# Sums of weight blocks made pair by pair, raw buffers reused in the order they come free, one bias load on another queue

## The chip, the core and the metric

The kernel runs on one core of a Trainium2 chip. The metric is the device time of one execution in microseconds (us). The kernel before was run three times; a fourth execution was profiled.

## What is computed

A streaming encoder with two layers, 512 frames of 1024 features, all in fp32. Cut to what matters here:

```
for i in range(DEPTH):                       # 2 layers
    h = rmsnorm(x, norm1_g[i])
    z = h @ w_in[i] + b_in[i]                # q, k, v, o, gates of an mLSTM; q, k, v, g of a retention; two branch gates
    y_m = sigmoid(mo) * headnorm(mlstm(mq, mk, mv, mi, mf))
    y_r = silu(rg) * headnorm(retention(rope(rq), rope(rk), rv))
    x += (sigmoid(gm) * (y_m @ w_bm[i]) + sigmoid(gr) * (y_r @ w_br[i])) @ w_out[i]
    x += relu(rmsnorm(x, norm2_g[i]) @ w_ff1[i] + b_ff1[i]) ** 2 @ w_ff2[i] + b_ff2[i]
    x += sigmoid(rmsnorm(x, norm3_g[i]) @ w_pe_gate[i]) * (p[i] @ w_pe[i])
return rmsnorm(x, final_g)
```

## The kernel before

**Products.** Activations lie transposed: features on the 128 partitions, 512 frames along the row. Each fp32 factor is split into a high and a low part (`split`, L286: a copy on ScalarE gives the high part, a subtraction on VectorE the low one), and a product is three matmuls: high by high, high by low, low by high. All weights are streamed from HBM once. `unit_list` (L152) writes out by hand the order of 302 units, 151 per layer. A T8 unit is a 1024x128 slice of weights for one output tile (24 matmuls of 512 columns), four V units are a 1024x512 slice for values, and PAIR and WIDE units are 2x2 blocks of weights that are multiplied by a scheme with seven block products in place of eight. That scheme needs, beside the four given blocks B11, B12, B21 and B22, the sums t1 = B12 + B11 and t3 = B12 + B22, and for WIDE also t2 = t1 + B22 (`MADE`, L96).

**Sums of weights.** t1, t2 and t3 are made in HBM by DMAs that GpSimd issues. `groups` (L128) puts PAIR units that belong together into a group of four (of two in the group `gm`); each WIDE unit is a group of its own. `sum_steps` (L315) lists, for each of the 24 groups in the order of their use, a copy of the first block into the sum (`a` = 0) and an accumulating DMA of the second one (`a` = 1), each over the whole group: t1 copy, t3 copy, t1 add, t3 add, for WIDE also t2 copy and t2 add. A group of four pairs or a WIDE group moves 1 MB in one step, the group `gm` 512 KB. The rows of a transfer lie on 128 rows of the block (`flat`, L312) and are cut at 4096 bytes. `step` (L327) issues the next one and makes it wait for the last matmul handed out until then. `tick` (L336) decides when: each unit adds a credit worked out from its time and its own load (`TIME`, L107; T8 and V units count 5.45 us), and while the credit is not negative, a step is issued for 4.5 of credit per MB. `next_unit` (L343) calls it once per unit, `run_wide` (L510) also inside the unit.

**Loads.** `fill_raws` (L363) hands out the loads of raw weights in the order of use on SyncE's queue: 512 KB for T8, V and WIDE pieces, twice 256 KB for a PAIR piece. A raw tile has 128x1024 elements. Four of them rotate under one tag (`wr`, `RAWS` = 4), so that load n + 4 of that tag waits for the tile of load n. One more (`wrx`), in the pool `low`, is used for units before `w_out` of the running layer, one load at a time (`cur["more"]`). `prep_next` (L391) fills raws, then splits the next piece into its high and low parts; in PAIR units it also forms differences and sums in the raw tiles (L423, L426), and in WIDE units L430. `ready` (L433) keeps this two units ahead of the product (`LOOK`, `READY`). Loads, splits and products have a fixed order on each engine; a late load holds the splits behind it on ScalarE and VectorE.

**Around them.** `t8` (L448), `run_pair` (L474) and `run_wide` (L510) issue the matmuls of a unit. `values` (L741) computes mLSTM values; its bias row, spread over 128 partitions, is loaded on SyncE's queue (L744) into a temporary tile (six of them rotate), and VectorE adds it at L727. GpSimd's queue also carries the spill and the fetch of retention values (L1177, L1207), the loads of x before `w_out` (L1363), the causal masks of the mLSTM (L1032), the powers of the norms (L667, L1052, L1098) and the sums of squares (L653). `Norm.square` (L637) holds the sum of squares in a tile `ssum`, `Norm.spread` (L701) the spread factor in a tile `rb`, 128x512 each, in the pool `one`. At the start, 11 matmuls on a tile of ones (L915, `WARM`) precede the first product.

Of the kernel before, what the change touches and what calls it, by code (L numbers as in the profile page):

```python
# [35 lines left out]
F32 = mybir.dt.float32  # L36
# [16 lines left out]
UN = 1024  # L53
LOOK = 2
AHEAD = 250
WARM = 11
NTMP = 6
RAWS = 4
PIECES = 3
# [59 lines left out]
def is_wide(g):  # L119
    return g[1][:2] == "rv"  # L120
# [116 lines left out]
def build(ctx, tc, ins, out):  # L237
# [71 lines left out]
    def block(g, x):  # L309
        return given[g, x] if x in GIVEN else sums[g, x]  # L310

    def flat(a):  # L312
        return a.rearrange("a p q -> (a p q)").rearrange("(r w) -> r w", r=P)

    def sum_steps():  # L315

        out = []
        for g in index:
            out += [(g, "t1", 0), (g, "t3", 0), (g, "t1", 1), (g, "t3", 1)]
            if is_wide(g):  # L320
                out += [(g, "t2", 0), (g, "t2", 1)]
        return out

    steps = sum_steps()
    made = {g: 0 for g in index}

    def step():  # L327
        g, x, a = steps[at["step"]]
        at["step"] += 1
        made[g] += 1  # L330
        kw = {"accum_op": OP.add} if a else {}
        dma = gp.dma_start(flat(block(g, x)), flat(block(g, MADE[x][a])), max_dma_last_dim=4096, **kw)
# [21 lines left out]
    formed = {}  # L354

    room = unit_list(0).index(("T8", "w_out", 0, 0))
    cur["room"], cur["more"] = (), None

    def halves(n):

        return [slice(0, Q), slice(Q, UN)] if n == 1 else [slice(0, UN)]

    def fill_raws(most=RAWS + 1):  # L363
        while at["load"] < len(loads) and len(raws) + len(kept) < most:
            n, x = loads[at["load"]]
            r = None
            if n in cur["room"] and cur["more"] not in raws:
                cur["more"] = n, x
                r = cur["low"].tile([P, UN], F32, name=f"wr{at['load']}", tag="wrx", bufs=1)
            elif len(raws) - (cur["more"] in raws) >= RAWS:  # L370
                break
            raws[n, x] = r = r or wpool.tile([P, UN], F32, name=f"wr{at['load']}", tag="wr", bufs=RAWS)
            if x:
                _, g, p = units[n]
                assert made[g] == 2 * len(MADE_OF(g)), (g, made[g], at["unit"])
                if is_wide(g):
                    in_order("load", nc.sync.dma_start(r, block(g, x[0])[x[1]]))
                else:
                    for k, y in enumerate(PIECE[x]):
                        in_order("load", nc.sync.dma_start(r[:, k * Q:(k + 1) * Q], block(g, y)[p]))  # L380
            elif units[n][0] == "IF":
                eng = nc.sync if n else nc.scalar
                eng.dma_start(r[:, 0:64], ins["wif"][n * L // NU])
            else:
                w = ins["wstream"][at["whole"]]
                for c in halves(n):
                    in_order("load", nc.sync.dma_start(r[:, c], w[:, c]))
                at["whole"] += 1
            at["load"] += 1

    def prep_next():  # L391
        n, x = order[at["prep"]]
        at["prep"] += 1
        fill_raws()

        w = Q if x == "D" else UN
        pl = cur["last"] if n >= NU - LAST else wpool
# [20 lines left out]
        pieces[n, x] = out_  # L418
        if x == "A" or wide and x[0] == "t2":
            kept[n, x] = r  # L420
        elif x == "C":

            ve.tensor_tensor(raws[n, "B"][:, Q:], kept.pop((n, "A"))[:, Q:], r[:, :Q], OP.add)  # L423
        elif x == "B":

            ve.tensor_tensor(r[:, :Q], r[:, :Q], r[:, Q:], OP.add)  # L426
            formed[n, "D"] = r
        elif wide and x[0] == "B21":
            t = cur["br"].tile([P, UN], F32, name=f"t4{n}_{x[1]}", tag=("ph", "pl")[x[1]])
            ve.tensor_tensor(t, kept.pop((n, ("t2", x[1]))), r, OP.add)  # L430
            formed[n, ("t4", x[1])] = t

    def ready(k):  # L433
        while at["prep"] < min(len(order), k + 1):
# [39 lines left out]
    def run_pair(name, act, done):  # L474
# [5 lines left out]
        def product(x):  # L480
# [8 lines left out]
            for k in range(4):  # L489
# [4 lines left out]
                te.matmul(o, wh[:, s], l, start=False, stop=False, skip_group_check=True)  # L494
                cur["mm"] = te.matmul(o, wl[:, s], h, start=False, stop=e, skip_group_check=True)
            done(x, o)

        def last():
            product("P4")
# [113 lines left out]
    class Norm:  # L613


        def __init__(self, name, i, gain, act=None, j0=0, j1=NT):
# [20 lines left out]
        def square(self, k, x, add=None):  # L637
            w = self.n * P
            x = x[:, self.s]
            if self.sum is None:  # L640
                pl = cur["last"] if self.half else opool
                sq = pl.tile([P, w if self.half else T], F32, name=f"{self.name}sum", tag="ssum", bufs=1)[:, :w]
            else:
                sq = tmp(f"{self.name}sq{k}")[:, :w]
            ac.activation(sq, x, AF.Square)
# [55 lines left out]
        def spread(self):  # L701
# [11 lines left out]
            pl = cur["last"] if self.half else opool  # L713
# [198 lines left out]
    cur["room"] = range(room)  # L912
    n1 = Norm("l0n1", 0, "g1", acts(xa_pool, "l0n1"))
    warm = ps("warm")
    for _ in range(WARM):  # L915
# [14 lines left out]
    for i in range(L):  # L930
        act_side, ph_side = ("right", "left") if i == 0 else ("left", "right")
        xa = n1.act
        if i:
            cur["low"] = phase(f"low{i}", ph_side)
            cur["tmp"], cur["ntmp"] = cur["low"], NTMP
            cur["room"] = range(i * NU // L, i * NU // L + room)
        cur["br"] = phase(f"br{i}", ph_side)

        sel = cur["br"].tile([P, H, P], F32R, name=f"l{i}sel", tag="sel")[0:32 + H]
# [511 lines left out]
            ff1(b, p)  # L1451
        n2_pool.release()
        n3_pool = phase(f"n3{i}", act_side)
        n3 = Norm(f"l{i}n3", i, "g3", acts(n3_pool, f"l{i}n3"))


        pe = n3_pool.tile([P, KT, T], F32, name=f"l{i}pe", tag="pe")
# [26 lines left out]
        nn = ([Norm(f"l{i}n4{a}", i, "gf", None, 2 * a, 2 * a + 2) for a in range(2)] if last  # L1484
              else [Norm(f"l{i + 1}n1", i + 1, "g1", acts(xa_pool, f"l{i + 1}n1"))])

        def pe_evac(o, c, s, nn):
            w = s.stop - s.start
# [201 lines left out]
```

## Time and profile before

| | us |
|---|---|
| three runs | 2342.51, 2340.75, 2342.23 |
| median | 2342.23 |
| profiled execution, device time | 2342.72 |
| its span in the profile | 2341.0 |

Between the profiled execution's time and its span lie 1.7 us. The profile names engines PE (TensorE), PEld (its weight loads), DVE (VectorE), ACT (ScalarE), POOL (GpSimd) and SP (SyncE, which only issues DMAs); `L288` is line 288 of the kernel. Tiles carry the names of the program: `wr` is a raw tile of weights, `wh` and `wl` its parts, `s0t` to `s23t` the sums of the 24 groups, `l0` and `l1` the layers. DMA queue q0 is GpSimd's, q1 SyncE's, q10 ScalarE's. A row of the timeline gives start, duration, engine, line, what is written and read, the number of merged instructions, and in brackets the idle time before it with what ended it.

### The profile page before, as it was taken

What the parts mean: (1) busy time and instruction counts of PE and PEld (TensorE: products, weight loads), DVE (VectorE), ACT (ScalarE), POOL (GpSimd) and SP (SyncE); (2) the same over time, 40 slices, a digit from 0 to 9 for tenths busy, and PEclk for the clock granted to TensorE, in tenths of its full rate; (3) what the DMA queues carried; (4) which work ended last, traced back from release to release, by engine and by line L of the source; (5) the groups of instructions that cost most, each with busy time, mean ns of one, the idle gap of its engine ahead of it and who ended that gap; (6) DMA issues with size and microseconds to landing.
All of it is one profiled execution on the core that took longest, in us unless ns stands there. A gap on an engine that the chain in (4) does not pass through costs nothing.

```text
span 2341.0 us, 35229 instructions
## 1 busy us (share of the span) xinstructions
PE 2320.0 (99%) x13660; PEld 2055.5 (88%) x13660; DVE 1722.4 (74%) x2658; ACT 1223.2 (52%) x1771; POOL 243.5 (10%) x369
## 2 busy tenths in 40 slices
PE   9999999999999999999999999999999999999998
PEld 8788898898998898899888888998989988998997
DVE  7777766886675677678778777778957656776785
ACT  6756544554554445445557564454636445445464
POOL 2111100001002100001311110000000020000012
PEclk9999999999999999999999999999999999999999
DMA  6666776566688667777776645434343543432441
GB/s 207 172 175 161 227 221 197 183 197 204 181 235 266 191 199 194 197 215 189 203 219 175 173 129 185 139 119 158 122 144 110 161 153 99 127 108 92 136 124 54
DMA packets 146631, 394.89 MB, mean 169 GB/s; under 512 B 15376, under 2 KB 18832, under 8 KB 146464
## 3 DMA queue, kind: packets, MB, share of 16 engines
q1 hardware_dynamic: 99952, 247.77, 32.0%
q0 software_dynamic: 31104, 117.45, 20.8%
q10 hardware_dynamic: 15408, 27.43, 3.5%
q8 instruction: 107, 1.75, 0.3%
q14 instruction: 60, 0.49, 0.1%
HBM read 373.71 MB, written 123.73 MB: 212 GB/s over the span
## 4 chain that ended last, share of the span: by engine, by line
PE 87%; DVE 5%; issue 4%; DMA 2%; ACT 1%; POOL 0%; DVEq 0%; ACTq 0%; POOLq 0%; SPq 0%
PE l1f L444 2%; PE l0f L444 2%; PE l0f L445 2%; PE l1f L445 2%; PE l1f L446 2%; PE l0f L446 2%; PE l0br L444 1%; PE l1br L444 1%; PE l0br L446 1%; PE l1br L445 1%; PE l1br L446 1%; PE l0br L445 1%; DMA wr<-wpairs 1%; PE l0pg L444 1%; PE l1bm L444 1%
## 5 line engine op out<-in xcount | busy, mean ns | idle before, releaser
L287 ACT ACTIVATE wh<-wr 128x1024 fp32r<-128x1024 f32 (+1 forms) x223 | 231.2, 1043 | 282.3 <-issue 71.6
L288 DVE TENSOR_TENSOR wl<-wr,wh 128x1024 fp32r<-128x1024 f32 (+1 forms) x221 | 272.2, 1233 | 76.5 <-ACT wh L287 74.9
L287 ACT ACTIVATE wh_B<-wr 128x1024 fp32r<-128x1024 f32 x100 | 105.9, 1059 | 153.4 <-PE l0bm L445 13.1
L288 DVE TENSOR_TENSOR wl_B<-wr,wh_B 128x1024 fp32r<-128x1024 f32 x100 | 122.0, 1220 | 27.2 <-ACT wh_B L287 27.1
L287 ACT ACTIVATE wh_D<-wr 128x512 fp32r<-128x512 f32 x76 | 47.9, 631 | 127.5 <-DVE wr L426 67.6
L287 ACT ACTIVATE wh_C<-wr 128x1024 fp32r<-128x1024 f32 x76 | 80.3, 1056 | 63.6 <-issue 10.5
L288 DVE TENSOR_TENSOR wl_A<-wr,wh_A 128x1024 fp32r<-128x1024 f32 x76 | 92.8, 1221 | 20.2 <-ACT wh_A L287 20.2
L288 DVE TENSOR_TENSOR wl_C<-wr,wh_C 128x1024 fp32r<-128x1024 f32 x76 | 94.3, 1241 | 15.7 <-ACT wh_C L287 15.3
L287 ACT ACTIVATE wh_A<-wr 128x1024 fp32r<-128x1024 f32 x76 | 80.0, 1052 | 46.1 <-PE l1f L445 6.7
L444 PE MATMUL l0f<-l0n2h,wh 128*128 128x512 f32 x256 | 99.8, 390 | 0.0
L444 PE MATMUL l1f<-l1n2h,wh 128*128 128x512 f32 x256 | 99.8, 390 | 0.0
L446 PE MATMUL l1f<-l1n2h,wl 128*128 128x512 f32 x256 | 99.7, 389 | 0.0
L446 PE MATMUL l0f<-l0n2h,wl 128*128 128x512 f32 x256 | 99.7, 389 | 0.0
L445 PE MATMUL l0f<-l0n2l,wh 128*128 128x512 f32 x256 | 99.6, 389 | 0.0
L445 PE MATMUL l1f<-l1n2l,wh 128*128 128x512 f32 x256 | 99.6, 389 | 0.0
L288 DVE TENSOR_TENSOR wl_D<-wr,wh_D 128x512 fp32r<-128x512 f32 x76 | 52.4, 690 | 36.9 <-ACT wh_D L287 35.7
L423 DVE TENSOR_TENSOR wr<-wr,wr 128x512 f32<-128x512 f32 x76 | 52.1, 686 | 13.5 <-DMA wr<-wpairs 12.1
L446 PEld LDWEIGHTS l1f<-l1n2h,wl 128*128 128x128 f32 x256 | 48.0, 188 | 10.2
L446 PEld LDWEIGHTS l0f<-l0n2h,wl 128*128 128x128 f32 x256 | 48.0, 188 | 10.2
L444 PEld LDWEIGHTS l0f<-l0n2h,wh 128*128 128x128 f32 x256 | 48.1, 188 | 9.8
L445 PEld LDWEIGHTS l1f<-l1n2l,wh 128*128 128x128 f32 x256 | 48.1, 188 | 9.8
L444 PEld LDWEIGHTS l1f<-l1n2h,wh 128*128 128x128 f32 x256 | 48.1, 188 | 9.7
(5625 smaller groups left out, 8359.6 us busy)
## 6 DMA issues: line engine op xcount, KB each, us to landing
wr<-wstream SPq DMA_DIRECT2D x219, 512.0 KB, 4.3
wr<-wpairs SPq DMA_DIRECT2D x228, 256.0 KB, 2.9
wr<-wwide SPq DMA_DIRECT2D x24, 512.0 KB, 3.8
s0t<-wwide POOLq DMA_DIRECT2D x5, 1024.0 KB, 8.4
s4t<-wwide POOLq DMA_DIRECT2D x5, 1024.0 KB, 8.7
s12t<-wwide POOLq DMA_DIRECT2D x5, 1024.0 KB, 8.3
s16t<-wwide POOLq DMA_DIRECT2D x5, 1024.0 KB, 8.9
s1t<-wpairs POOLq DMA_DIRECT2D x4, 1024.0 KB, 8.1
```

The source lines that it names most:

```text
L287: a = ac.activation(hi_ap, src, AF.Copy)
L288: return a, ve.tensor_sub(lo_ap, src, hi_ap.bitcast(F32))
L423: ve.tensor_tensor(raws[n, "B"][:, Q:], kept.pop((n, "A"))[:, Q:], r[:, :Q], OP.add)
L444: te.matmul(o, sh, mh, start=first, stop=False)
L445: te.matmul(o, sh, ml, start=False, stop=False)
L446: cur["mm"] = te.matmul(o, sl, mh, start=False, stop=last)
```

## The change

The steps of a sum go over one pair (256 KB) or over one half of a WIDE group (512 KB) in place of a whole group, with the adding steps one pair behind the copies: 352 steps in place of 104. A step costs 1.13 of credit per 256 KB. `pace` issues at most one step each time; it is called by `tick`, after the fourth of a T8 unit's eight slices, and after each block product of a PAIR unit. A load waits for the steps of its own pair only. The four raw tiles get tags of their own and go to the next load in the order in which the program has given them back, the tile `wrx` likewise; from each layer's first WIDE unit up to its `w_out`, the norm's tile (`nr`, 128x1024, which now holds the sum of squares and the spread factor side by side, and passes from norm to norm) serves as one raw tile more. The bias row of the first layer's first values is issued from GpSimd. `WARM` is 13.

```diff
-WARM = 11
+WARM = 13
-STEP, SHARE = 4.5, 0.7
+STEP, SHARE = 1.13, 0.7
...
-        for g in index:
-            out += [(g, "t1", 0), (g, "t3", 0), (g, "t1", 1), (g, "t3", 1)]
+        for g, v in groups().items():
+            n = 2 if is_wide(g) else len(v)
+            for p in range(n + 1):
+                out += [(g, x, 0, p) for x in ("t1", "t3") if p < n]
+                out += [(g, x, 1, p - 1) for x in ("t1", "t3") if p]
             if is_wide(g):
-                out += [(g, "t2", 0), (g, "t2", 1)]
+                out += [(g, "t2", a, p) for a in range(2) for p in range(n)]
...
-        dma = gp.dma_start(flat(block(g, x)), flat(block(g, MADE[x][a])), max_dma_last_dim=4096, **kw)
+        at["credit"] -= STEP * (2 if is_wide(g) else 1)
+        dma = gp.dma_start(flat(block(g, x)[p:p + 1]), flat(block(g, MADE[x][a])[p:p + 1]), max_dma_last_dim=4096,
+                           **kw)
...
+    def pace():
+        if at["step"] < len(steps) and at["credit"] >= 0:
+            step()
...
-        while at["step"] < len(steps) and at["credit"] >= 0:
-            at["credit"] -= STEP * len(groups()[steps[at["step"]][0]]) / 4 if not is_wide(steps[at["step"]][0]) else STEP
-            step()
+        pace()
...
+    wide0 = unit_list(0).index(("WIDE", (0, "rv0"), 0))
+    where = {n + i * NU // L: ("low", "one") if n >= wide0 else ("low",) for i in range(L) for n in range(room)}
+    free, taken = ["low", "one"] + list(range(RAWS)), {}
+    def norm_tile():
+        return opool.tile([P, 2 * T], F32, name="nr", tag="nr", bufs=1)
+    def raw_tile(a):
+        if a == "one":
+            return norm_tile()
+        pl, tag = (cur["low"], "wrx") if a == "low" else (wpool, f"wr{a}")
+        return pl.tile([P, UN], F32, name=f"wr{at['load']}", tag=tag, bufs=1)
...
+            fits = where.get(n, ()) if n * L // NU == cur["layer"] else ()
+            a = next((a for a in free if a in range(RAWS) or a in fits), None)
+            if a is None:
                 break
...
+        def give(*a):
+            free.extend(taken.pop(k) for k in a)
...
+        elif x == "D":
+            give((n, "B"))
         elif x == "C":
             ve.tensor_tensor(raws[n, "B"][:, Q:], kept.pop((n, "A"))[:, Q:], r[:, :Q], OP.add)
+            give((n, "A"), (n, "C"))
...
             if k == 3:
                 flush()
+                pace()
...
-            self.b = pl.tile([P, w if self.half else T], F32, name=f"{n}rb", tag="rb", bufs=1)[:, :w]
+            self.b = self.own[:, T:T + w]
...
-        nc.sync.dma_start(bvt, bv_ap)
+        (gp if nm == "l0m0" else nc.sync).dma_start(bvt, bv_ap)
```

More of the change, by code (lines that the diff above doesn't have):

```diff
@@ L356, in build, with fill_raws @@
     room = unit_list(0).index(("T8", "w_out", 0, 0))
[L357 removed]
+    wide0 = unit_list(0).index(("WIDE", (0, "rv0"), 0))
[8 more added lines that the diff above has]
+        return pl.tile([P, UN], F32, name=f"wr{at['load']}", tag=tag, bufs=1)
     def halves(n):
         return [slice(0, Q), slice(Q, UN)] if n == 1 else [slice(0, UN)]
[L363 to L364 removed]
+    def fill_raws(most=None):
+        while at["load"] < len(loads) and at["load"] != most:
             n, x = loads[at["load"]]
[L366 to L370, printed above, removed]
+            fits = where.get(n, ()) if n * L // NU == cur["layer"] else ()
+            a = next((a for a in free if a in range(RAWS) or a in fits), None)
+            if a is None:
                 break
[L372 removed]
+            free.remove(a)
+            taken[n, x] = a
+            raws[n, x] = r = raw_tile(a)
             if x:
                 _, g, p = units[n]
[L375 removed]
+                assert made.get((g, x[1] if is_wide(g) else p)) == 2 * len(MADE_OF(g)), (g, p, made, at["unit"])
                 if is_wide(g):
@@ L640, in square @@
             if self.sum is None:
-                pl = cur["last"] if self.half else opool
-                sq = pl.tile([P, w if self.half else T], F32, name=f"{self.name}sum", tag="ssum", bufs=1)[:, :w]
+                if self.half:
+                    sq = cur["last"].tile([P, w], F32, name=f"{self.name}sum", tag="ssum", bufs=1)
+                else:
+                    self.own = self.own or norm_tile()
+                    sq = self.own[:, 0:w]
             else:
@@ L911, in build @@
     cur["tmp"], cur["ntmp"] = cur["low"], NTMP
-    cur["room"] = range(room)
+    cur["layer"] = 0
     n1 = Norm("l0n1", 0, "g1", acts(xa_pool, "l0n1"))
```

22 lines of the change are left out of this document (13 added, 9 removed).

## The prediction, made before the change was run

> **What bounds the kernel now.** I read the page first, then busy time by stage, then TensorE's waits, then the same work in both layers, then what ended the idle time of the engines that feed TensorE.
>
> ```profile
> span 2341.0 us, 35229 instructions
> PE 2320.0 (99%) x13660; PEld 2055.5 (88%) x13660; DVE 1722.4 (74%) x2658; ACT 1223.2 (52%) x1771; POOL 243.5 (10%) x369
> ```
>
> ```profile
> 0.00:60.00 60.00, 58.13 (x261) 48.48 (x262) 43.95 (x74) 37.88 (x52) 17.69 (x48) 1.00 0.61 208
> 660.00:720.00 60.00, 60.00 (x377) 54.26 (x376) 39.40 (x54) 29.45 (x42) 6.13 (x9) 1.00 0.86 253
> 2280.00:2341.00 61.00, 51.63 (x327) 46.57 (x325) 35.80 (x69) 27.31 (x55) 13.05 (x17) 0.92 0.19 60
> ```
>
> TensorE is busy for 2320.0 of 2341.0 us, and the change takes no product away. So at most 21 us can go, and 9.4 of them (61.00 less 51.63) lie in the last stage, where no sum and no raw buffer plays a part, and 1.9 in the first. The DMA engines are not the bound either: where their share is highest of these rows (0.86), TensorE is busy for 60.00 of 60 us. Some 10 us remain in between. TensorE's waits from 30 to 1150 us (total, times, longest) say what ended most of them:
>
> ```profile
> PE l0bgm L446 <- DVE wl L288: 1.6, 1, 1.6
> PE l0r1brqa L493 <- DVE l0r1brqy L570: 1.4, 1, 1.4
> PE l0o22a L493 <- DVE l0x L1415: 1.2, 1, 1.2
> PE l0r0vc L537 <- DVE wl_t L288: 0.7, 1, 0.7
> PE l0r2o1a L493 <- DVE l0r2o1y L570: 0.4, 1, 0.4
> ```
>
> All name VectorE, and all are in layer 0. Layer 1 does the same products, so it is the yardstick (first and last start, of the norms' sums and of one transposition):
>
> ```profile
> L660 PE MATMUL l0n1ss<-ones_r,l0n1sum x8: 165/251/251, 23.2 to 23.9; 128*128 128x2 f32 x8
> L660 PE MATMUL l0n3ss<-ones_r,l0n3sum x8: 165/251/251, 1131.3 to 1132.0; 128*128 128x2 f32 x8
> L660 PE MATMUL l1n1ss<-ones_r,l1n1sum x8: 165/251/251, 1185.5 to 1186.2; 128*128 128x2 f32 x8
> L660 PE MATMUL l1n3ss<-ones_r,l1n3sum x8: 165/251/251, 2286.7 to 2287.4; 128*128 128x2 f32 x8
> ...
> L814 PE MATMUL l0r0ot<-ident,l0r0num x16: 270/272/273, 425.5 to 432.4; 128*128 128x128 f32 x16
> L814 PE MATMUL l1r0ot<-ident,l1r0num x16: 270/272/273, 1580.9 to 1587.8; 128*128 128x128 f32 x16
> ```
>
> From n1ss to r0ot layer 0 takes 425.5 - 23.2 = 402.3 us, layer 1 takes 395.4: 6.9 more in layer 0. From r0ot to n3ss both take 705.8. So 6.9 us is what layer 0's early part loses, and the question is to what. VectorE's and ScalarE's idle time ahead of three of those waits, with the steps of sums that GpSimd had just issued:
>
> ```profile
> 66.89 0.75 DVE L727 SCALAR_TENSOR_TENSOR l0m0v<-l0m0vp,l0n1rc,l0m0bv 128x512 f32<-128x512 f32 x1 [4.35 <-DMA l0m0bv<-bv]
> 388.62 0.69 DVE L423 TENSOR_TENSOR wr<-wr,wr 128x512 f32<-128x512 f32 x1 [4.13 <-DMA wr<-wpairs]
> 1022.96 1.06 ACT L287 ACTIVATE wh_B<-wr 128x1024 fp32r<-128x1024 f32 x1 [4.48 <-DMA wr<-wpairs]
> ```
>
> ```profile
> 57.88 0.98 POOL L332 DMA_DIRECT2D s0t<-wwide  x1 [7.89 <-PE l0m0vp L759]
> 378.75 0.90 POOL L332 DMA_DIRECT2D s5t<-wpairs  x1 [15.33 <-PE l0r0s L446]
> 1010.63 0.88 POOL L332 DMA_DIRECT2D s16t<-wwide  x1 [8.24 <-PE l0o20a L495]
> ```
>
> ```profile
> 58.51 8.36 DMA l0m0bv<-bv
> ...
> 1012.24 10.61 DMA wr<-wpairs
> ```
>
> ```profile
> wr<-wpairs SPq DMA_DIRECT2D x228, 256.0 KB, 2.9
> s1t<-wpairs POOLq DMA_DIRECT2D x4, 1024.0 KB, 8.1
> s2t<-wpairs POOLq DMA_DIRECT2D x4, 512.0 KB, 5.4
> ```
>
> The pattern is one: a step of 1 MB is issued, a small transfer follows within 0.6 to 5 us, and the small one lands as late as the step does. In the chain of waits, the bias took 8.36 us and a 256 KB load 10.61, against a median of 2.9 for its kind. The reader is to see that the collision is chance (the median load meets none) and that TensorE pays for it only where the next split was due at once.
>
> **The change part by part.** I sum against the profiled execution, 2342.7 us (span 2341.0 and 1.7 around it); the median of the runs shown is 0.5 lower.
>
> *Smaller steps.* The landing of 1 MB (8.1) and 512 KB (5.4) puts 256 KB, continued on the same line, at 5.4 - 1.35 = 4.1 us, an estimate. A transfer caught in it is held for at most that, in place of 8 to 10 us, though there are more than three times as many steps to meet. For the loads at 388.6 and 1023.0 the hold shrinks by 4 us or more, which is the idle time of 4.13 and 4.48 they caused, so I take both waits as gone: -1.4 and -1.2 (between 0 and these). What is late next is the split itself, one 1.2 us instruction of VectorE, with work queued ahead of it. The step at 57.88 belongs to a WIDE group and becomes 512 KB; it stays ahead of the bias. The wait of 0.7 follows VectorE work, not a load: -0.3. The rest of the 6.9 (less 1.6, 1.4 and 0.7, so 3.2) is spread over waits too small for that view; I take a third, -1.0, between 0 and all.
>
> *The bias.* It moves from SyncE's queue to GpSimd's. The tile that it fills was free only at 58.5, when VectorE had read the old content, so it is issued no earlier. Behind a 512 KB step in the same queue it lands near 58.5 + 5.4 = 63.9 instead of 66.9, and VectorE's 4.35 us of idle time become 1.4. TensorE's 1.6 us and the smaller waits around it come from VectorE's queue, which runs nearly without a pause from there on. I take -2.0; 0 if another step stands ahead, -3 if the bias goes first. SyncE loses nothing by it: its next load waited for a raw tile. On GpSimd the bias, waiting for its tile, holds the steps and the masks queued behind it.
>
> *Buffers.* In layers 0 and 1 a PAIR load waited for a raw tile that VectorE gave back late, as this chain of layer 0 shows:
>
> ```profile
> 613.62 0.70 DVE wl_D L288
> 614.34 2.69 DMA wr<-wpairs
> 617.15 0.18 DVE wr L423
> ```
>
> The wait of 0.4 above follows from it. With one raw tile more in that stretch, and none that must wait its turn, the load can start before the split ends. I take -0.4 in each layer, -0.8 (0 to -1.5). After `w_out` four tiles remain and the order in which they come back is nearly that of their rotation: 0. The norm's tile is idle in that stretch, and its next writer comes after `w_out`'s first tile: 0.
>
> *Two more warm matmuls.*
>
> ```profile
> 6.93 0.80 PE L972 MATMUL l0if<-l0n1h,wh 128*128 128x512 f32 x1 [0.82 <-DVE wh L288]
> 9.66 0.63 PE L973 MATMUL l0if<-l0n1l,wh 128*128 128x512 f32 x1
> 10.75 0.40 PE L446 MATMUL l0m0z<-l0n1h,wl 128*128 128x512 f32 x1
> ```
>
> ```profile
> 22.19 0.68 DVE L651 TENSOR_TENSOR l0n1sum<-l0n1sum,l0n1sq 128x512 f32<-128x512 f32 x1
> ```
>
> The eight matmuls from 6.93 to 10.5 take 0.63 us and start 0.43 apart, later ones 0.40 and 0.23, although the row of that stage gives a clock of 1.00. If the eight ran at the later pace, 8 x 0.2 = 1.6 us would go. But n1ss, at 23.2 now, needs the sum that VectorE ends at 22.9, with no part in the warm-up: of 1.6 us, 0.3 get through. I take -0.3 (0 to -1.6). The Trainium skill, "TensorE: Matmul & The Clock Gate", Part 1, says that the array runs at half rate until a free-running window of about 3.4 us has been busy throughout. The slow matmuls here agree with it in size; by that rule the window that held the gap of 0.82 us would count as busy after the change, and the full 1.6 would be at stake.
>
> *More issues.* 352 steps against 104 are 248 more instructions on GpSimd.
>
> ```profile
> L332 POOL DMA_DIRECT2D s2t<-wpairs x4: 533/750/863, 161.3 to 178.5; - x4
> ```
>
> At 0.53 for a copy and 0.86 for an add, the 248 cost 248 x 0.7 = 174 us of GpSimd, which is busy for 243.5 of 2341 us. It stays far from a bound, but a mask, a power or a fetch of values can now find it inside an issue, by up to 0.9 us, and small loads meet small steps oftener. I take +1.5, between 0 and +4: the lower end if VectorE's slack covers every case, the upper one if four places as tight as the listed waits pay 1 us each.
>
> The sum: -1.4 - 1.2 - 0.3 - 1.0 - 2.0 - 0.8 - 0.3 + 1.5 = -5.5, so 2337.2 by the profile's time and 2336.7 by the median. I say 2337.
>
> **The rivals.** *All of it is recovered.* Layer 0 becomes as quick as layer 1 (-6.9), with -1.2, -0.8 and the start's -0.3, and the new issues cost nothing: 2342.7 - 9.2 = 2333.5. For it: layer 1 reaches that pace with steps of 1 MB running in its first part. Against it: there the collisions missed by chance, and short ones will be many.
>
> *The collisions only change shape.* The same bytes pass the same engines, each load is held a little and often, and the bias stays behind a step. Then only buffers and start remain: 2342.7 - 1.1 = 2341.6. The Trainium skill, "DMA: Bandwidth & Descriptors", "Queues, rings and completion order", says that each DMA engine goes round the queues packet by packet; by that, the size of a step would not hold a load from another queue for its whole length, and smaller steps would win nothing. The load of 10.61 us speaks against it.
>
> *Slower: steps that don't get through.* The rows of a 256 KB step are 2 KB. The program hands out about two such steps per T8 unit of 5.45 us, so each has 2.7 us of all DMA engines. These are queue 0's packets, MB and share, in three windows: an add of 1 MB from 1359.8 to 1366.8, a copy from 1321.4 to 1325.2, and spills with rows of 2 KB from 1440 to 1446.
>
> ```profile
> q0 software_dynamic: 271, 1.05, 84.1%
> ```
>
> ```profile
> q0 software_dynamic: 271, 1.05, 89.8%
> ```
>
> ```profile
> q0 software_dynamic: 320, 1.05, 45.1%
> ```
>
> The add takes 0.841 x 7.0 = 5.9 us of all engines per MB, 1.5 per 256 KB; the copy 3.4 per MB; the spills, with 2 KB rows, 2.7 per MB. So short rows cost no more by the nearest row, but that row is between SBUF and HBM. If a 2 KB row of an add cost what a 4 KB one does, a step would need 2.9 us. That is over 2.7, the point from which queue 0 falls behind; bias, fetched values and rows of x queue up in it, and loads share the engines with sums without a pause. Layer 0's loss of 6.9, made with sums half that long, would come once more: 2342.7 + 6.9 = 2349.6.
>
> **How the numbers follow.** Two times of this kernel can be told apart from about 0.2%, 4.7 us: faster is below 2337.5, slower above 2346.9. The forecast gets 0.48 (0.31 below 2337.5, as its spread of 2334.5 to 2339.5 lies across that line), full recovery 0.14, the change of shape 0.18, the slow queue 0.20. So faster 0.45, same 0.35, slower 0.20. The range of 2333 to 2348 holds the first three cases but for a few hundredths of the second, and the near part of the last.
>
> **What would show it.** Right: VectorE's idle time ahead of l0m0v below 2 us; no wait at l0r1brqa and l0o22a; the difference between the layers from n1ss to r0ot below 3 us; steps that land within about 5 us; GpSimd near 420 us busy. Wrong: adds of 256 KB that land later than 8 us, waits of TensorE that follow masks or fetched values, or the same waits at other tiles of layer 0. If n1ss comes at 21.6, the start's bound was not VectorE's.

## The result and the profile after

The changed kernel takes 2344.23 us (median of 20 runs, 2339.84 to 2348.78); the kernel before took 2340.72 us in the same comparison (20 runs, 2337.24 to 2342.51). The ratio is 1.0018, with a 95% interval from 1.0012 to 1.0023: slower by some 4 us, where the prediction had said 2337 and faster. The time lies inside the stated range of 2333 to 2348, but by none of the ways that the range was made for. The profiled execution of the changed kernel took 2342.84 us, with a span of 2341.1, so the two traces are equally long; what one gained the other lost elsewhere.

The page of the changed kernel, its span and busy times, and TensorE's three stages of the prediction:

```profile
span 2341.1 us, 35757 instructions
PE 2319.3 (99%) x13664; PEld 2056.1 (88%) x13664; DVE 1723.5 (74%) x2658; ACT 1222.7 (52%) x1771; POOL 402.3 (17%) x618
```

```profile
0.00:60.00 60.00, 58.94 (x271) 49.12 (x272) 45.39 (x76) 39.17 (x54) 21.84 (x51) 1.00 0.63 211
660.00:720.00 60.00, 60.00 (x386) 54.66 (x385) 39.71 (x54) 27.88 (x42) 15.99 (x24) 1.00 0.88 239
2280.00:2341.00 61.00, 51.54 (x328) 46.48 (x326) 35.85 (x69) 27.71 (x56) 13.10 (x17) 0.95 0.20 61
```

GpSimd's 402.3 us come close to the forecast's 420. TensorE is as busy as before; the idle time has moved. Its waits in the changed kernel, over the whole span (total, times, longest):

```profile
PE l0r3o1a L521 <- DVE l0r3o1y L599: 2.7, 1, 2.7
PE l1r0o0c L521 <- ACT l1r0o0y L591: 1.8, 1, 1.8
PE l1r3o1a L521 <- DVE l1r3o1y L599: 1.5, 1, 1.5
PE l0r0o0c L521 <- ACT l0r0o0y L591: 1.5, 1, 1.5
...
PE l0r0vc L566 <- DVE wl_t L288: 0.7, 1, 0.7
PE l0bgm L473 <- DVE wl L288: 0.7, 1, 0.7
...
PE l1r0vc L566 <- DVE wl_t L288: 0.5, 1, 0.5
```

The waits at `l0r1brqa` and `l0o22a` are gone, that at `l0bgm` fell from 1.6 to 0.7, that at `l0r0vc` is what it was, and `l1r0vc` has one of 0.5. In their place stand four waits, and they come in pairs: `r3o1a` and `r0o0c`, in layer 0 and in layer 1. Layer 1's were made at 1566 and 1805 us, when no sum runs any more (the last step is issued at 1413 us), so the sums aren't their cause. The yardstick of the prediction shows the same:

```profile
L693 PE MATMUL l0n1ss<-ones_r,nr x8: 251/251/272, 21.7 to 22.5; 128*128 128x2 f32 x8
L693 PE MATMUL l1n1ss<-ones_r,nr x8: 165/251/251, 1181.5 to 1182.2; 128*128 128x2 f32 x8
L846 PE MATMUL l0r0ot<-ident,l0r0num x16: 270/272/273, 420.8 to 427.7; 128*128 128x128 f32 x16
L846 PE MATMUL l1r0ot<-ident,l1r0num x16: 270/272/273, 1580.4 to 1587.3; 128*128 128x128 f32 x16
```

From n1ss to r0ot layer 0 now takes 399.1 us (402.3 before) and layer 1 takes 398.9 (395.4 before). The difference between the layers is gone, half of it because layer 1 became slower.

Steps of sums land sooner, as the DMA issues show (median us from issue to landing at the end; the groups of pairs lie between 3.6 and 5.0), and the bias lands before VectorE has long waited for it:

```profile
s0t<-wwide POOLq DMA_DIRECT2D x10, 512.0 KB, 6.0
s1t<-wpairs POOLq DMA_DIRECT2D x16, 256.0 KB, 4.1
```

```profile
63.76 0.75 DVE L759 SCALAR_TENSOR_TENSOR l0m0v<-l0m0vp,l0n1rc,l0m0bv 128x512 f32<-128x512 f32 x1 [0.74 <-DMA l0m0bv<-bv]
```

**What makes the wait at `r3o1a`.** The end of the chain of waits ahead of it in layer 1, and VectorE's timeline there:

```profile
1803.79 0.16 DVE wr L446
1803.95 0.45 issue
1804.39 0.43 DVE l1r3o1y L599
1804.82 0.04 issue
1804.87 0.39 PE l1r3o1a L521
```

```profile
1801.80 0.42 DVE L597 TENSOR_TENSOR l1r3o1y<-l1r3o1c,l1r3o1y 128x256 f32<-128x256 f32 x1
1803.79 0.69 DVE L446 TENSOR_TENSOR wr<-wr,wr 128x512 f32<-128x512 f32 x1 [1.57 <-DMA wr<-wpairs]
1804.39 0.42 DVE L599 TENSOR_TENSOR l1r3o1y<-l1r3o1a,l1r3o1y 128x256 f32<-128x256 f32 x1
```

L446 prepares the third piece of a PAIR unit: it adds A and C from two raw tiles. The reader is to see that this add, which nobody needs yet, stands on VectorE between two evictions and waits 1.57 us for a load, while TensorE waits for the eviction behind it. In the kernel before, the same two evictions (L568 and L570) stand next to each other:

```profile
1803.01 0.42 DVE L568 TENSOR_TENSOR l1r3o1y<-l1r3o1c,l1r3o1y 128x256 f32<-128x256 f32 x1
1803.72 0.42 DVE L570 TENSOR_TENSOR l1r3o1y<-l1r3o1a,l1r3o1y 128x256 f32<-128x256 f32 x1 [0.29 <-PE l1r3o1a L495]
```

The splits of the weights are held in their order by hand; the raw add isn't. The add writes a tile `wr`, while the split of B that comes behind it, at 1806.05 us, reads `nr`, the norm's tile: the add belongs to the next pair, and stands ahead of the last splits of the pair before it. That it was placed there because one tile more lets its loads be handed out, and expected, earlier is my explanation of this order; no run here shows the expectation. On the chip the load came 1.57 us after VectorE was free for the add.

### The profile page after: what moved, and what is told of

Same layout as the page of the kernel before. It is cut to its first block, busy times and chain, and to the rows that moved or that the text cites. A ratio compares the mean times of both kernels' runs of the same rounds, so it can differ in the third digit from the quotient of the medians.

```text
span 2341.1 us, 35757 instructions
## 1 busy us (share of the span) xinstructions
PE 2319.3 (99%) x13664; PEld 2056.1 (88%) x13664; DVE 1723.5 (74%) x2658; ACT 1222.7 (52%) x1771; POOL 402.3 (17%) x618
## 4 chain that ended last, share of the span: by engine, by line
PE 88%; DVE 5%; issue 2%; DMA 2%; ACT 1%; POOL 1%; DVEq 0%; ACTq 0%; POOLq 0%; SPq 0%
PE l1f L471 2%; PE l0f L471 2%; PE l0f L472 2%; PE l1f L472 2%; PE l1f L473 2%; PE l0f L473 2%; PE l0br L471 1%; PE l1br L471 1%; PE l1br L472 1%; PE l0br L473 1%; PE l1br L473 1%; PE l0br L472 1%; PE l0pg L471 1%; PE l1bm L471 1%; PE l0pg L473 1%
## 5 line engine op out<-in xcount | busy, mean ns | idle before, releaser
L287 ACT ACTIVATE wh<-wr 128x1024 fp32r<-128x1024 f32 (+1 forms) x213 | 221.3, 1043 | 283.9 <-issue 69.6
L288 DVE TENSOR_TENSOR wl<-wr,wh 128x1024 fp32r<-128x1024 f32 (+1 forms) x211 | 260.1, 1234 | 70.8 <-ACT wh L287 70.4
L287 ACT ACTIVATE wh_B<-wr 128x1024 fp32r<-128x1024 f32 x86 | 91.0, 1059 | 114.3 <-PE l1bm L472 8.8
L288 DVE TENSOR_TENSOR wl_B<-wr,wh_B 128x1024 fp32r<-128x1024 f32 x86 | 105.0, 1221 | 18.3 <-ACT wh_B L287 18.1
L287 ACT ACTIVATE wh_D<-wr 128x512 fp32r<-128x512 f32 x66 | 41.6, 631 | 118.1 <-DVE wr L450 51.7
L287 ACT ACTIVATE wh_C<-wr 128x1024 fp32r<-128x1024 f32 x66 | 69.8, 1057 | 62.1 <-issue 9.6
L288 DVE TENSOR_TENSOR wl_C<-wr,wh_C 128x1024 fp32r<-128x1024 f32 x66 | 82.2, 1246 | 18.6 <-ACT wh_C L287 18.0
L288 DVE TENSOR_TENSOR wl_D<-wr,wh_D 128x512 fp32r<-128x512 f32 x66 | 45.5, 690 | 32.3 <-ACT wh_D L287 31.1
L686 POOL TENSOR_TENSOR nr<-nr,l1n3sq 128x512 f32<-128x512 f32 x6 | 9.2, 1540 | 330.8 <-ACT nr L678 309.8
```

The source lines that it names most:

```text
L287: a = ac.activation(hi_ap, src, AF.Copy)
L288: return a, ve.tensor_sub(lo_ap, src, hi_ap.bitcast(F32))
L686: (add or gp).tensor_tensor(self.sum, self.sum, sq, OP.add)
```

## The experiments

A difference below is the median against the median of the kernel before on the same chip (2338.1 to 2339.8 us), with the 95% interval of the ratio. The runs lie on four chips, and an interval is some 2 us to either side: two rows less than about 3 us apart can't be told apart by their times alone.

| run | what it is | us | ratio |
|---|---|---|---|
| e1_sums | before + small steps | -3.2 | 0.9976 to 0.9994 |
| e5_buf | before + raw buffers | +7.6 | 1.0021 to 1.0046 |
| e6_warm | before + 2 warm matmuls | +1.8 | 1.0001 to 1.0019 |
| e2_oldbuf | after, old raw buffers | -0.6 | 0.9985 to 1.0002 |
| e3_noone, e14_noone | after, without the norm's tile | -1.2, -2.6 | 0.9986 to 1.0004, 0.9979 to 0.9996 |
| e13_after | after, again | +3.9 | 1.0012 to 1.0030 |
| e4_tie, e8_floor | after, raw add tied | +15.6, +6.3 | 1.0053 to 1.0078, 1.0022 to 1.0051 |
| f1_bias, f2_warm | small steps + bias, + 13 warm | -3.9, +1.7 | 0.9977 to 0.9994, 0.9996 to 1.0014 |
| f3_noone_w11 | after, no norm's tile, 11 warm | -3.8 | 0.9979 to 0.9997 |
| e9_late, e10_sums_late | e2_oldbuf, e1_sums, fourth split late | -2.6, -2.8 | 0.9981 to 0.9999, 0.9985 to 1.0003 |
| g1_dup, g2_w9 | f3_noone_w11, products added; 9 warm | -1.7, -2.3 | 0.9985 to 1.0003, 0.9980 to 0.9997 |

**The parts by themselves.** `e1_sums` is the kernel before with `sum_steps`, `step`, `pace` and `STEP` of the change. 

> The kernel before with one part of the change alone: sums pair by pair in steps of 256 KB. Old raw buffers, bias on SyncE's queue, 11 warm matmuls. Theory (the sums pay as forecast, the loss is made by the raw buffers): the waits at l0r1brqa and l0o22a go, 1.7 and 1.4 us by the two traces, nothing is lost at l0r3o1a and l1r3o1a, so some 3 us below the kernel before. Rival (the 248 issues on GpSimd and the many small transfers take back what the small steps give): level with the kernel before or up to 4 us above, with waits of TensorE behind masks or fetched values in layer 0 only.

It came out at -3.2 us, as the theory had it, without waits at l0r1brqa, l0o22a and r3o1a; the wait at l0r0vc is gone too. `e2_oldbuf` is the changed kernel with the old `fill_raws` and the norm's tiles `ssum` and `rb`. 

> The changed kernel with the old rule for raw buffers and the norm's two tiles apart again; small steps, bias on GpSimd's queue and 13 warm matmuls stay. Theory (the buffers make the loss): the add of the next pair no longer stands ahead of the eviction of l0r3o1y and l1r3o1y on VectorE, the losses of 2.7 and 1.6 us there are gone, and the 5.4 us gained by 617 us stay: 5 us below the kernel before, 8 below the changed one. Rival (the steps make it): it stays within 2 us of the changed kernel.

The two waits were gone, and its profiled execution took 2333.1, but the median was only 0.6 below the kernel before, with runs from 2333 to 2341. So the buffers made a loss (4 us of it by the medians), and something else did as well. `e3_noone`:

```diff
-    where = {n + i * NU // L: ("low", "one") if n >= wide0 else ("low",) for i in ...}
+    where = {n + i * NU // L: ("low",) for i in ...}
```

> The changed kernel without the norm's tile as a raw buffer; tiles are still taken as they come free. Theory (it is the sixth tile that lets the next pair's raw add move ahead of the eviction): both waits at r3o1a go, 4.3 us below the changed kernel or a little more. Rival (any free order of the tiles does it): the wait stays, within 1 us of the changed kernel.

Both waits were gone and the median was 1.2 below the kernel before. The comparison was made again on one chip with the changed kernel itself. 

> The changed kernel, unchanged, profiled once more and timed on the same chip as the next one. Theory: the waits at l0r3o1a and l1r3o1a come back in every execution (2 to 3 and 1 to 2 us), as the order on VectorE is fixed; the waits at r0o0c vary by a microsecond, as the landing of the fetch does. Rival (all of it is the luck of one execution): the waits at r3o1a are gone in this profile. Time 2 to 5 us above the kernel before.

> The changed kernel without the norm's tile as a raw buffer, again, now on the same chip as the changed kernel itself. Theory (the sixth tile alone makes the loss): 4 to 5 us below the changed kernel, and level with the kernel before to 2 us below it. Rival: within 2 us of the changed kernel.

2343.12 against 2336.64: the norm's tile costs 6.5 us here (4.7 by the earlier runs, on other chips). The changed kernel's second profile has the waits again, and the one without the tile hasn't (first rows of TensorE's waits, the changed kernel, then without the tile):

```profile
PE l0r3o1a L521 <- DVE l0r3o1y L599: 2.3, 1, 2.3
PE l1r0o0c L521 <- ACT l1r0o0y L591: 1.9, 1, 1.9
PE l0r0o0c L521 <- ACT l0r0o0y L591: 1.7, 1, 1.7
PE l1r3o1a L521 <- DVE l1r3o1y L599: 1.3, 1, 1.3
```

```profile
PE l1r0o0c L521 <- ACT l1r0o0y L591: 2.1, 1, 2.1
PE l0r0o0c L521 <- ACT l0r0o0y L591: 1.7, 1, 1.7
```

The waits at `l0r0vc` and `l1r0vc` (0.7 and 0.5) are in both profiles of the changed kernel too and in neither of those without the tile, so they are part of its price; what makes them wasn't followed. A sixth tile of its own, in place of the norm's, was not tried.

And the new buffers on the kernel before, with its sums of 1 MB. 

> The kernel before with the new rule for raw buffers alone (six tiles taken as they come free); sums, bias and warm matmuls as before. Theory (the hoisted add makes the loss): TensorE waits at l0r3o1a and l1r3o1a for 1.5 to 2.7 us each behind an add that waits for its load, so 3 to 4 us above the kernel before. Rival (the loss needs the small steps as well): no such waits, and 0 to 1 us below the kernel before, as the prediction had it.

It is 7.6 us slower, and its waits begin with these:

```profile
PE l1r3o1a L513 <- DVE l1r3o1y L590: 2.7, 1, 2.7
PE l0r3o1a L513 <- DVE l0r3o1y L590: 2.5, 1, 2.5
```

So the buffers make the loss without any small step. The same run holds a surprise: the waits at `l0r1brqa` and `l0o22a`, which the small steps were to remove, are gone here too, under steps of 1 MB. The raw add near `l0r1brqa`, in e1_sums and then in e5_buf:

```profile
381.57 0.69 DVE L430 TENSOR_TENSOR wr<-wr,wr 128x512 f32<-128x512 f32 x1 [1.28 <-DMA wr<-wpairs]
```

```profile
379.62 0.69 DVE L439 TENSOR_TENSOR wr<-wr,wr 128x512 f32<-128x512 f32 x1
```

Small steps leave it where it was, between two evictions, and shorten its wait from 4.13 us to 1.28. The new buffers give VectorE another order, in which the add there finds its loads done. So the wait at `l0r1brqa`, whose row the prediction shows (388.62, L423), has the mechanism of `r3o1a`: a raw add ahead of an eviction, waiting for a load. The change moved it from one place of the kernel to two others. Either part of the change removes the wait, and it can be gained only once.

**Holding the add by hand.** `e4_tie` and `e8_floor` leave the buffers and give L446 a place:

```diff
+            add = ve.tensor_tensor(raws[n, "B"][:, Q:], ...)
+            tc.add_manual_dep(add.ins, cur["prep"][1].ins.name, ORDER, ...)   # e4: its own C
+            tc.add_manual_dep(add.ins, cur["floor"][1].ins.name, ORDER, ...)  # e8: the pair before
```

> The changed kernel with one order added: a pair's raw add on VectorE comes after the split of that pair's own C. No buffer, transfer or wait is taken away. Theory (VectorE's order alone makes the loss, early loads do no harm): both waits at r3o1a go or shrink to a few tenths, as the pair's own add of 0.69 us now stands there, 3 to 4 us below the changed kernel. Rival (the loads collide, the order only shows it): TensorE waits as long at the same places, behind the splits instead, and the time stays within 1 us.

> The changed kernel with a looser order than the first tie: a pair's raw add comes after the last split of the pair before, and may come ahead of its own pair's splits. Theory (only the add that overtakes a whole pair does harm; the first tie lost because the third piece then had to wait for the add): no waits at r3o1a, none of the new ones at o22a, o23a, o32a and o33a, 4 us below the changed kernel. Rival (any order held by hand costs): again above the changed kernel.

Both removed the waits at r3o1a and both lost elsewhere: +15.6 and +6.3. In e4_tie TensorE waits for 0.6 to 1.0 us at six products of `w_out`, behind VectorE's additions to x; in e8_floor it waits at 19 places, 15 of them for 0.2 to 0.7 us. These waits add up to 10.4 us, less than the changed kernel's 14.2; TensorE's busy time is what is longer (2324.6 against 2319.3 us), so the price of that order hides in rows that count as busy. One order given by hand changes where the rest of VectorE's work is placed; which of its moves cost what wasn't followed. The theory's half on the place of the add stands; that holding it by hand is free does not.

**What is left: the value fetch.** The runs without the norm's tile kept waits of 1.6 to 2.6 us at `r0o0c`. In layer 1 of the changed kernel ScalarE's timeline shows what the eviction stands behind:

```profile
1561.51 0.36 ACT L589 ACTIVATE l1r0o0y<-l1r0o0a 128x256 f32<-128x256 f32 x1
1561.78 1.40 ACT L287 ACTIVATE l1r1vh<-l1r1vl 128x512 fp32r<-128x512 f32 x2
1564.68 0.63 ACT L287 ACTIVATE l1r1vh<-l1r1vl 128x512 fp32r<-128x512 f32 x1 [1.50 <-DMA l1r1vl<-rv_spill]
1565.22 0.36 ACT L591 ACTIVATE l1r0o0y<-l1r0o0c 128x256 f32<-128x256 f32 x1
```

The split of the fourth fetched value tile waits 1.50 us for its transfer, and the eviction L591 waits behind it. Two runs put that split behind the eviction, one on e2_oldbuf, one on e1_sums:

```diff
+            if x == "P5" and late:
+                tc.add_manual_dep(late.pop()()[0].ins, e.ins.name, ORDER, reason="eviction first")
```

> The run with the old raw buffers (small steps, bias on GpSimd's queue, 13 warm matmuls) and one order more: ScalarE's split of the fourth fetched value tile comes after the eviction of the second product of r0o0 and r2o0, so that eviction no longer stands behind a fetch. Theory (what is left of the loss, and the scatter from run to run, is the late fetch at r0o0c with the half-rate stretch that can follow a wait of that length): the waits of 1.8 and 1.6 us at l0r0o0c and l1r0o0c go, the runs lie closer together than 8 us, and the median is 3 to 5 us below that of the run with the old raw buffers, some 5 below the kernel before. Rival (the scatter comes from elsewhere): the median stays within 1 us of that run's and the scatter too.

> The run with the small steps alone, with the same order more on ScalarE. Theory: its waits at r0o0c were 1.1 and 1.0 us in the profile, so 2 us less than that run, some 5 below the kernel before. If bias and warm matmuls are worth the 1 us that the traces show, the run with them is 1 us better than this one. Rival (bias and warm matmuls cost 2.6 us, as the medians of the first runs say): this one is 2 us or more better than the run with them.

With the order the waits at r0o0c fell to 1.2 and 0.6 (e9_late) and 0.9 and 0.3 (e10_sums_late), and e9_late came to -2.6, where e2_oldbuf had -0.6; the runs lay between 2332 and 2339. That is 2 us of the 3 to 5 forecast, with intervals that overlap; the third tile's split waits too (0.97 and 0.49 us). e10_sums_late, at -2.8, is no better than e1_sums. So the fetch seems to matter where bias and warm matmuls are changed, and why was still open.

**How much of the profile of before was luck.** The kernel before was profiled twice more. 

> The kernel before, unchanged, profiled once more. Theory (three of the waits that the prediction sold as gains belong to the one execution that was profiled): the eight products at the start run at the quick pace although there are 11 warm matmuls, so the first sum of squares comes near 21.7 us and not 23.2, and the profiled time is near 2340, not 2342.7. Rival (the waits belong to the kernel): the first sum of squares at 23.2 again, and TensorE's waits at l0r1brqa (1.4) and l0o22a (1.2) again. Each of the three is judged by itself.

> The kernel before, unchanged, a third profile, for the same question: which of its waits come back in every execution. Theory: the waits at l0r1brqa and l0o22a, which hang on when a 1 MB step is issued, come back; the slow start doesn't. Rival: all come back, or none.

The first of these, TensorE's first products and its first sum of squares:

```profile
6.93 0.50 PE L972 MATMUL l0if<-l0n1h,wh 128*128 128x512 f32 x1 [0.81 <-DVE wh L288]
7.27 0.39 PE L973 MATMUL l0if<-l0n1l,wh 128*128 128x512 f32 x1
7.50 0.40 PE L444 MATMUL l0m0z<-l0n1h,wh 128*128 128x512 f32 x1
```

```profile
L660 PE MATMUL l0n1ss<-ones_r,l0n1sum x8: 251/251/272, 22.0 to 22.8; 128*128 128x2 f32 x8
```

The same gap of 0.8 us, and no slow products: 22.0 here and 21.6 in the other, where the profile that I argued from had 23.2. The start's 1.5 us belonged to that execution. The Trainium skill, "TensorE: Matmul & The Clock Gate", Part 1, says as much: the window runs free, so the number of cold products varies from run to run. The traces agree: 23.2, 22.0 and 21.6 us in three executions of one kernel. The wait at `l0r1brqa` came back both times (1.3 and 1.2), that at `l0o22a` once (0.8), that at `l0bgm` both times (1.7 and 1.4).

**Two warm matmuls, 400 us later.** The DMA view of the changed kernel counts 107 transfers of code on a queue of their own (packets, MB, share of 16 engines):

```profile
q8 instruction: 107, 1.75, 0.3%
```

TensorE has 2 x 13664 instructions with its weight loads, and over 107 these are 255 for each 16 KB, so I take the queue for TensorE's. The Trainium skill, "Runtime: NRT & Kernel Launch", "Instruction fetch mechanics", gives 256 instructions to a block of 16 KB, which agrees, and calls the crossing mostly hidden; no wait of TensorE listed here names its code. In the DMA view of layer 1 of the changed kernel, one such load falls into the third microsecond after r0o0a begins (1561.65 to 1562.65):

```profile
q8 instruction: 1, 0.02, 8.0%
```

8.0% of 16 engines for 1 us is 1.28 us of one engine, and that is by how much the packets of the fetch on one engine could fall behind, an estimate. In all three profiles of the kernel before there is none in that microsecond, in either layer: it comes 3.2 to 4.0 us after r0o0a. Two warm matmuls more (four matmul instructions and their weight loads) move every later boundary by eight instructions. But the bias adds a transfer to the queue of the fetches, so both were tried alone. 

> The kernel before with 13 warm matmuls in place of 11 and nothing else. Theory (the two matmuls move TensorE's later code loads by their instructions, so that one falls on the value fetch in both layers): the waits at l0r0o0c and l1r0o0c rise from 0.7 to 1.0 us to 1.5 to 2.0, the code load comes 2 to 3 us after r0o0a begins, the start is no better than in the other traces with 11, and the time is 1 to 3 us above the kernel before. Rival (the transfer on GpSimd's queue does it): waits of 0.7 to 1.0, level with the kernel before, or 0.3 below it as predicted.

> The run with the small steps alone, and the bias on GpSimd's queue; 11 warm matmuls, old raw buffers. Theory (matmuls move the code load, the bias is a gain): waits at r0o0c of 0.7 to 1.1, the wait at l0bgm 0.7 in place of 1.7, 1 us better than the run with the small steps alone, some 4 below the kernel before. Rival (the bias moves the fetches): waits of 1.5 to 2.6 at r0o0c, 1 us worse than that run.

> The run with the small steps alone, and 13 warm matmuls; bias on SyncE's queue, old raw buffers. Theory: waits at r0o0c of 1.5 to 2.6 and the code load early, l0bgm 1.7, so 2 us worse than the run with the small steps alone, level with the kernel before or 1 below it. Rival: waits of 0.7 to 1.1, level with that run (3 below).

> The changed kernel without the norm's tile as a raw buffer and with 11 warm matmuls. Theory (these two are all that the change lost): no wait at r3o1a, 0.7 to 1.1 at r0o0c, 1 to 2 us below the same with 13 matmuls, some 4 below the kernel before. Rival (the waits at r0o0c come from the bias or the free order of the tiles): level with the same with 13 matmuls, 1 to 2 below the kernel before.

```diff
-WARM = 13
+WARM = 11
```

With 13 warm matmuls the small steps give +1.7, with 11 and the bias moved -3.9: 5.6 us between them on one chip, for both differences together. The two matmuls alone make the kernel before 1.8 us slower (interval 1.0001 to 1.0019). And the changed kernel without the norm's tile and with 11 is at -3.8, its runs between 2334.7 and 2338.0. TensorE's waits there:

```profile
PE l0r0o0c L521 <- ACT l0r0o0y L591: 1.1, 1, 1.1
...
PE l1r0o0c L521 <- ACT l1r0o0y L591: 0.3, 1, 0.3
```

Not all agrees. In e6_warm the load came into the third microsecond only in layer 0 (wait 1.7), not in layer 1 (wait 0.9), where I had expected both. In layer 0 of f1_bias the wait was 2.3 with the code load late (5.2 us after r0o0a): there sums share the queue with the fetch, and a second cause must exist. The last two runs moved the code loads in another way, both on f3_noone_w11:

```diff
+                for _ in range(3 if (n, j) == ("l1n1", 0) else 1):
                     te.matmul(o[:, 2 * j:2 * j + 2], self.sum[:, s], ones[:, 0:2], ...)
```

> The version with 11 warm matmuls and without the norm's tile as a raw buffer, with one product of layer 1's first norm (l1n1ss, near 1183 us) done three times over in place of once: the same values are written again, and TensorE has as many instructions more as with 13 warm matmuls, but only from there on. Theory (where a code load falls decides): at l0r0o0c the wait stays near 1 us and the code load at 3.2 us or later after r0o0a begins; at l1r0o0c the load comes at 2.1 to 2.9 us and the wait is 1.5 us or more. The time is 1 to 3 us above that version's (4 below the kernel before), so 1 to 3 below it. Rival (warm matmuls act otherwise): both waits stay near 1 us or below, and the time is that version's, 0.3 us for the products added.

> The same version with 9 warm matmuls. Theory: the code loads come later still after r0o0a begins, so no wait at r0o0c is over 1.2 us; at the start nothing is lost that the 11 gave beyond a few tenths, so level with that version, some 4 us below the kernel before. Rival (every step away from 11 costs): 1 to 3 us above that version.

In g1_dup layer 0 is the control. Its waits, and the code load of layer 1 in the third microsecond after r0o0a (1560.36 to 1561.36); in layer 0 there is none in that microsecond:

```profile
PE l1r0o0c L521 <- ACT l1r0o0y L591: 2.4, 1, 2.4
...
PE l0r0o0c L521 <- ACT l0r0o0y L591: 1.1, 1, 1.1
```

```profile
q8 instruction: 1, 0.02, 8.3%
```

The wait appears in the layer whose code was moved and not in the other: 2.4 us in layer 1, against 0.3 in f3_noone_w11. The time is -1.7 where f3_noone_w11 had -3.8, but the intervals overlap. With 9 warm matmuls the loads come late, the waits are 1.4 and 0.9, the first above the 1.2 that the theory allowed, and the time is -2.3, with a wait of 2.0 and eight slow products at the start; whether that is worse than with 11 the intervals don't tell.

The fetch itself shows it better than the wait, which also hangs on what else ScalarE has to do. In the 20 profiles, two layers each, the fourth tile landed 4.7 to 5.8 us after r0o0a began in the 20 cases where a code load began 2.1 to 2.9 us after it. In the 20 cases where the load began later (3.2 to 5.3) the tile landed at 3.5 to 4.6, but for the 5.5 of f1_bias. And it follows the load, not the number of warm matmuls: in layer 1 of e6_warm (13, load at 3.7) it landed at 4.1, in layer 1 of g1_dup (11, load at 2.1) at 5.6. In e8_floor TensorE waited for only 0.6 and 0.7 us although the tiles landed at 5.2 and 4.9. That an early code load goes with a fetch that lands about 1 us later is shown; that its packets stand in the fetch's way is argued from the times.

## Why the prediction was wrong, step by step

- *Smaller steps* (-1.4, -1.2, -0.3, -1.0, and +1.5 for the issues, so -2.4): -3.2 by themselves, with all three waits gone. The step holds in size. Its reason holds only in part: the waits at `l0r1brqa` and `l0o22a` go with the new buffers as well, that at `l0o22a` is missing from one of three profiles of the kernel before, and that at `l0r0vc` came back with the norm's tile.
- *The bias* (-2.0): VectorE's idle time fell below 2 us, as said, but TensorE's wait only from 1.6 to 0.7, and by the medians of f1_bias and e1_sums, on two chips, it is worth 0.7, which their intervals don't tell from nothing. The mechanism was right and the term too large by half or more.
- *Buffers* (-0.8): **this is the step that failed.** It said that "the load can start before the split ends", and put the price of the norm's tile as a raw buffer at 0. The gain came: the waits at `r2o1a` are gone from the changed kernel. But with that tile another add stands first on VectorE, and TensorE waits behind it for 2.7 and 1.5 us, at `r0vc` for 0.7 and 0.5. By the medians the tile costs 6.5 us, and the new buffers on the kernel before +7.6 where -0.8 was forecast. I costed a buffer by the wait that it removes and didn't ask which instructions only the old scarcity had held back.
- *Two more warm matmuls* (-0.3): the second failure, in sign. The 1.5 us at the start weren't the kernel's, and n1ss came at 21.7, so by the prediction's own sign VectorE's sum wasn't the bound there. The two cost 1.8 us alone; with the small steps more, up to 5.6 with the bias's move counted in. The longer waits that come with them lie near 405 and 1562 us.
- *The rivals*: the queue didn't fall behind, since 256 KB land in 3.6 to 5.0 us by the medians, and layer 0 didn't lose its 6.9 once more. The short rows that it feared don't show in the traces: every data packet of GpSimd's queue has 4096 bytes, before and after, and so have those of the spills that I took for rows of 2 KB. The slower end came by another mechanism than the one that I had priced.
- *The signs*: all that I had named for "right" came true (0.74 us ahead of l0m0v, two waits gone, layers 0.2 us apart, 256 KB steps within 5 us by their medians, the slowest 8.1, and 402 us of GpSimd), and so did one for "wrong", waits at other places of layer 0. They told of the step that held and not of the time.
- *The list of waits.* "All name VectorE" was wrong. Between `l0o22a` and `l0r0vc` the view has one more row, which the prediction leaves out, and it is the place of two of the four new waits:

```profile
PE l0r0o0c L493 <- ACT l0r0o0y L562: 0.8, 1, 0.8
```

That all were in layer 0 followed from the window, which ends ahead of layer 1.

Together: the small steps and the bias at -3.9, the norm's tile at +6.5 and the warm matmuls at +1.2 to +3.3 (f3_noone_w11 against e14_noone, f1_bias against e2_oldbuf) make +3.8 to +5.9; the changed kernel measured +3.5 and +3.9. With intervals of some 2 us on each term, that is consistent and no proof.

Why the medians lose more than the waits: some waits of TensorE are followed by products at half pace. The rows behind the wait of 2.4 us in g1_dup, where the starts go from 0.12 to 0.21 us apart:

```profile
1565.46 0.28 PE L522 MATMUL l1r0o0c<-l1xsl,wh_C 128*128 128x256 f32 x1
1565.58 0.35 PE L523 MATMUL l1r0o0a<-l1xsh,wl_B 128*128 128x256 f32 x1
1565.72 0.42 PE L521 MATMUL l1r0o0a<-l1xsh,wh_B 128*128 128x256 f32 x1
1565.94 0.42 PE L522 MATMUL l1r0o0a<-l1xsl,wh_B 128*128 128x256 f32 x1
```

This lasts some 3 us there (16 products, 1.5 us lost). The granted clock, the third number from the end, shows it in that stretch (0.50):

```profile
1565.64:1569.04 3.40, 3.40 (x18) 3.40 (x18) 1.71 (x4) 1.15 (x3) 0.00 (x0) 0.50 0.00 0
```

In the 20 profiles of this study 27 waits are of 1.6 us or more, and 12 of them, of 1.8 to 2.5 us, are followed by such a stretch of 3.4 us; which ones are varies between executions of one kernel (none behind l0r3o1a in the first profile of the changed kernel, one in the second). A stretch lowers the mean clock of a whole run by only 0.0007 (3.41 x 0.5 / 2341), but the scatter follows it: in e2_oldbuf the five runs with a mean clock of 0.997 took 2337.5 to 2341.4 us, the six with 0.998 or 0.999 took 2333.0 to 2338.9.

## What to carry to other kernels

A wait found in one profile may be that execution's own: before it is counted as a gain, look for it in a second profile of the same kernel. Of every buffer that is added, ask which instruction its early load lets the program place ahead of work that is due: on an engine that keeps its order, an early add that waits for a load can be worse than a late one. And even two matmuls at the start can move later code loads onto a transfer that something waits for, so a small edit is timed by itself.

## What the hardware showed that I had not expected

What I take for TensorE's code comes in 107 loads of 16 KB; one takes about 1 us of one DMA engine (median 0.97 us in the 20 profiles, 0.88 to 2.27). Where one began within a fetch of four 256 KB transfers, the last of them landed 4.7 to 5.8 us after r0o0a began; where it began later, at 3.5 to 4.6, but for one at 5.5. A wait of 1.6 to 2.7 us on TensorE was followed by 3.4 us at a granted clock of 0.50 in 12 of 27 cases; a window laid on the stretch shows it, the mean over the run hardly does.
